# Attention outputs instead of softmax weights divided by the sums, with the reciprocals transposed on TensorE, in an encoder layer on one core

## The chip, the core and the metric

The kernel runs on one core of a Trainium2 chip. It has a matrix engine (TensorE, PE in the profile, with its weight loads as PEld), a vector engine (VectorE, DVE), a scalar engine (ScalarE, ACT), a general one (GpSimd, POOL), an engine that only issues transfers here (SyncE, SP), and 16 DMA engines. The metric is the device time of one execution, in microseconds (us).

## What is computed

One layer of an encoder in float32 for two requests, a prompt of 1024 tokens and a sample of 512, each of 1024 features, with tokens on a grid 64 columns wide (16 and 8 rows): normalization, attention of each query to a neighbourhood of up to 8 rows by 16 columns of keys, a residual, then normalization, a SwiGLU feed-forward of 2816 features, a residual and a last normalization. The attention has 16 heads of 64 features. Cut to what matters, per row of queries (rs is its first row of keys; kr and vr are 8 rows of keys and values in column bands of 32):

```python
s = einsum('bjqhd,bkjchd->bhjqkc', qr, kr) * scale
s = where(valid_j, s + bias, -inf)
p = softmax(s over all keys k, c)
return einsum('bhjqkc,bkjchd->bjqhd', p, vr)      # then o @ w_o
```

A softmax is exp(s - max) divided by its sum over the keys. That sum is one number for a query and a head, so the division can be made on the weights p, or later on the 64 outputs of that query and head.

## The kernel before

**Stages.** Until about 160 us tokens are normalized and transposed and the values V of all heads are projected, and stored in device memory. Then come the attention steps of the prompt (179 to about 520 us), those of the sample (to about 730 us) with the output projection between them, and then the feed-forward, which the change does not touch. Every float32 operand of a large product is split into a rounded part and a remainder (`split`, L138 on ACT and L139 on DVE; with a scale L141 and L142) and multiplied in three passes.

**A step.** A step is one pair of heads, one group of query rows and one of four blocks of 16 columns: 128 queries (8 rows by 16 columns) by 384 keys in the prompt, by 256 in the sample. The prompt has 8 pairs x 2 groups x 4 blocks = 64 steps, the sample 8 x 4 = 32. In a step

- `scores` multiplies queries by keys (pss, L394, 6 products on PE), adds the bias and finds the maximum (s and mx, L402, DVE, straight from PSUM), takes the exponential with its sum (s and sm, L405, ACT), inverts the sum (ri, L407, DVE) and multiplies the weights s by it, for head 0 on DVE (L409) and for head 1 on ACT (L411);
- `flip` transposes the weights on PE in blocks of 128x128 (ptt, L420, 3 per head in the prompt, 2 in the sample), copies the result rounded (pT, L423, ACT) and puts the remainder beside it (L424, DVE);
- `weighted` multiplies by V (po, L431): the outputs stand in PSUM with the features of a head on the partitions and the queries along the free axis, one bank per head and two steps beside each other;
- `collect`, every second step, adds the parts of po (tmp, L441 on ACT and L442 on DVE; oT, L444 on DVE) into oT, [128 features of two heads, 512 queries]; after the last block of a group a POOL transfer stores oT in device memory (o_d, L461).

**The order on the engines.** `step` (L476) writes the work of neighbouring steps interleaved: the scores of step t+1, the transposes of step t, then pieces of other products that keep PE busy, then the value products of step t. These pieces (`fillers`) are the q and k projections of the next pair (pg, L332, 12 products for a step), and in the sample also the output projection (pgo, L586). After each step `chores.do()` splits one piece that has been loaded (V of a row group: v from vr, four transfers at L378 on SP; weights of the next projection: whl from wr) and starts the next load; the buffers for these loads ("raw") are two, shared by both kinds, so a load starts only after the work on the one before. `fill_bias` keeps the bias tiles three ahead (bp, bs: transfers on SP, and for the prompt a memset on POOL, L204 and L208). The final order on each engine is set by the tile scheduler from this program and its estimates of durations; it, not only the text, moves rows when an instruction is added. PSUM has eight banks: two each for pss, ptt, po and pg.

## Time and profile before

| | |
|---|---|
| three timed runs | 1843.49, 1845.11, 1845.51 us (median 1845.11) |
| the profiled execution | 1845.18 us, span 1843.4 us |
| PE, PEld busy | 1754.1, 1522.5 us (95%, 83%) |
| DVE, ACT, POOL busy | 1192.9, 863.7, 448.4 us (65%, 47%, 24%) |
| mean DMA traffic | 151 GB/s |

Busy times are means over stages with different limits. In the views below L402 is line 402 of the kernel; "out<-in" are the program's names; a time "idle before" is how long the engine stood still before an instruction, and the name behind "<-" is what it waited for last. Windows give the busy time of each engine in a stretch of the span; the chain of waits follows the work that ended last back from instruction to releaser.

### The profile page before, as it was taken

The numbers are of one execution on the slowest core, as the hardware profiler recorded it, in microseconds if no ns is written. First come the engines' busy times: TensorE is split into PE (matmuls) and PEld (weight loads), VectorE is DVE, ScalarE is ACT, GpSimd is POOL, SyncE is SP. The second block draws the span as 40 slices with busy tenths as digits, with TensorE's granted clock in tenths as the row PEclk, the third lists the DMA queues.
The fourth block names the chain that finished last, engine by engine and source line by source line (L and its number), as shares of the span: only waits on it lengthen the run. The fifth ranks groups of instructions, "written<-read, shape, count | busy, mean of one in ns | idle before, by whom it ended". The sixth has DMA issues, their size and how long they took to land.

```text
span 1843.4 us, 25648 instructions
## 1 busy us (share of the span) xinstructions
PE 1754.1 (95%) x9178; PEld 1522.5 (83%) x9178; DVE 1192.9 (65%) x2191; ACT 863.7 (47%) x1706; POOL 448.4 (24%) x495
## 2 busy tenths in 40 slices
PE   8999999999999999979999999999999969999898
PEld 6877777777767777868999999899999958887676
DVE  4401877777896566768777777867777444545654
ACT  4411776766785554544443444444443333333322
POOL 1211000000130000112243342424243323526420
PEclk9999999999999999988999999999999979999999
DMA  7755334333464443676343434544333277635732
GB/s 245 221 183 160 111 105 113 108 101 103 126 208 146 133 149 100 221 247 185 108 121 118 133 110 151 164 129 125 108 120 107 68 272 245 225 130 191 232 129 100
DMA packets 222048, 278.80 MB, mean 151 GB/s; under 512 B 25600, under 2 KB 171776, under 8 KB 221920
## 3 DMA queue, kind: packets, MB, share of 16 engines
q1 hardware_dynamic: 201824, 210.69, 37.3%
q0 software_dynamic: 18368, 60.18, 9.5%
q10 hardware_dynamic: 1728, 6.29, 1.1%
q8 instruction: 72, 1.18, 0.3%
q14 instruction: 56, 0.46, 0.1%
HBM read 213.20 MB, written 76.43 MB: 157 GB/s over the span
## 4 chain that ended last, share of the span: by engine, by line
PE 68%; DVE 10%; DMA 9%; ACT 5%; issue 3%; SPq 2%; POOL 2%; DVEq 0%; ACTq 0%; POOLq 0%
PE pa L754 20%; PE pd L910 12%; PE pd L754 10%; PE pgv L278 7%; PE pg L332 6%; PE pb L754 5%; DMA vr<-v_d 5%; PE pgo L586 3%; DMA dr<-ffn_w_down 2%; PE pss L394 2%; PE ptt L420 2%; DVE pT L424 2%; SPq L378 2%; PE po L431 2%; ACT s L405 1%
## 5 line engine op out<-in xcount | busy, mean ns | idle before, releaser
L910 PE MATMUL pd<-wd,go 128*128 128x512 f32 x1386 | 323.0, 395 | 30.5 <-ACT go L138 20.4
L910 PEld LDWEIGHTS pd<-wd,go 128*128 128x128 f32 x1386 | 263.0, 191 | 90.4 <-ACT go L138 21.6
L754 PE MATMUL pa<-h,ws 128*128 128x384 f32 x1056 | 201.8, 339 | 2.9 <-ACT c L777 2.1
L754 PE MATMUL pa<-h,wa 128*128 128x384 f32 x1056 | 195.1, 338 | 7.0 <-ACT wa L138 4.5
L754 PE MATMUL pd<-h,ws 128*128 128x384 f32 x1056 | 198.3, 335 | 1.2 <-ACT h L138 0.6
L332 PE MATMUL pg<-hTp,whl 128*128 128x512 f32 x768 | 193.7, 399 | 0.0
L754 PEld LDWEIGHTS pa<-h,wa 128*128 128x128 f32 x1056 | 185.8, 190 | 8.9 <-ACT wa L138 5.2
L139 DVE TENSOR_TENSOR ws<-wt,ws 128x1024 fp32r<-128x1024 f32 x88 | 108.6, 1235 | 127.1 <-ACT ws L138 126.7
L754 PEld LDWEIGHTS pa<-h,ws 128*128 128x128 f32 x1056 | 185.1, 189 | 6.7 <-ACT c L777 4.3
L754 PEld LDWEIGHTS pd<-h,ws 128*128 128x128 f32 x1056 | 184.5, 188 | 1.8 <-ACT h L138 1.0
L332 PEld LDWEIGHTS pg<-hTp,whl 128*128 128x128 f32 x768 | 139.9, 188 | 27.5 <-issue 0.4
L805 POOL DMA_DIRECT2D gop_d<-c x66 | 50.5, 765 | 387.4 <-DVE c L796 380.3
L405 ACT ACTIVATE s<-s,mx 128x384 f32<-128x384 f32 (+1 forms) x192 | 110.7, 580 | 67.3 <-DVE mx L402 67.1
L586 PE MATMUL pgo<-wo,oh 128*128 128x512 f32 x576 | 139.3, 392 | 0.2 <-DVE oh L139 0.2
L139 DVE TENSOR_TENSOR wa<-wr,wa 128x512 fp32r<-128x512 f32 x132 | 117.8, 897 | 18.4 <-ACT wa L138 17.8
L138 ACT CAST ws<-wt 128x1024 fp32r<-128x1024 f32 x88 | 92.6, 1053 | 68.6 <-PE pd L754 65.4
L586 PEld LDWEIGHTS pgo<-wo,oh 128*128 128x128 f32 x576 | 105.6, 188 | 20.7 <-DVE oh L139 0.6
L138 ACT CAST go<-gr 128x1408 fp32r<-128x1408 f32 x42 | 57.7, 1374 | 131.2 <-PE pd L910 114.0
L138 ACT CAST wa<-wr 128x512 fp32r<-128x512 f32 x132 | 81.4, 621 | 62.8 <-PE pb L754 40.0
L754 PE MATMUL pb<-h,wa 128*128 128x384 f32 x528 | 102.0, 340 | 3.4 <-DVE c L774 3.4
L332 PE MATMUL pg<-hTs,whl 128*128 128x512 f32 x384 | 102.6, 404 | 0.8 <-DVE q L343 0.8
L424 DVE TENSOR_TENSOR pT<-ptt,pT 128x384 fp32r<-128x384 f32 (+1 forms) x192 | 90.0, 507 | 17.3 <-ACT pT L423 16.5
(138 smaller groups left out, 2859.6 us busy)
## 6 DMA issues: line engine op xcount, KB each, us to landing
gr<-gop_d SPq DMA_DIRECT2D x42, 704.0 KB
dr<-ffn_w_down SPq DMA_DIRECT2D x99, 256.0 KB
wr<-ffn_w_gate SPq DMA_DIRECT2D x44, 512.0 KB
wr<-ffn_w_up SPq DMA_DIRECT2D x44, 512.0 KB
wr<-na_w_qkv SPq DMA_DIRECT2D x38, 512.0 KB
gop_d<-gs POOLq DMA_DIRECT2D x88, 192.0 KB, 4.4
gop_d<-c POOLq DMA_DIRECT2D x66, 192.0 KB, 2.8
vr<-v_d SPq DMA_DIRECT2D x192, 64.0 KB
```

What stands on the lines that cost most here:

```text
L138: nc.scalar.copy(hi, raw)
L139: nc.vector.tensor_tensor(lo, raw, f32(hi), ALU.subtract)
L278: nc.tensor.matmul(pg, hh[a][:, k, c:c + P], wv[k // 2][b][:, k % 2], start=(k == 0 and i == 0), stop=(k == KB - 1 and i == 2))
L332: nc.tensor.matmul(pg, w[:, a, k, :], h[b][:, k, c:c + 512], start=(k == 0 and i == 0), stop=(k == KB - 1 and i == 2))
L378: nc.sync.dma_start(out=raw[:, j * P:(j + 1) * P], in_=src[:, BS[j]:BS[j] + 32, :])
L394: nc.tensor.matmul(pt[:, :n], q[h * HD:(h + 1) * HD, a, j].rearrange("p r i -> p (r i)"), kv[:, krow:krow + nrow, BS[j]:BS[j] + 32], start ...
L405: nc.scalar.activation(s[:, :n], s[:, :n], AF.Exp, bias=mx, scale=-1.0, accum_out=sm)
L424: nc.vector.tensor_tensor(pT[:, :n, 1], pv, f32(pT[:, :n, 0]), ALU.subtract)
L586: nc.tensor.matmul(pg, ohs[k // 4][:, a, k % 4], wo[:, b, k, n * 512:(n + 1) * 512], start=(k == 0 and i == 0), stop=(k == KB - 1 and i == 2))
L754: nc.tensor.matmul(bank[:, :HT], a(y, k), b[:, z, k], start=start and k == 0 and i == 0, stop=k == KB // 2 - 1 and i == 2, skip_group_chec ...
L805: nc.gpsimd.dma_start(out=gop_d[i, 3 * c:3 * c + 3, :, p].rearrange("j q t -> q j t"), in_=a.rearrange("q (j t) -> q j t", j=3))
L910: nc.tensor.matmul(pd, go[:, y, i], wds[i][:, z], start=(i == 0 and m == 0), stop=(i == NP - 1 and m == 2))
```

## The change

The weights s are no longer multiplied by the reciprocal. The sums of both heads go into the two columns of one tile sm; one reciprocal on DVE reads them 64 times each and writes ri, [128 queries, 2 x 64]. `flip` transposes ri after the transposes of head 1, into the free last quarter of the same PSUM bank: column by column it becomes [2 x 64 features, 128 queries], with the reciprocal of head 0 on partitions 0 to 63 and of head 1 on 64 to 127, which is the layout of oT. ACT copies it to rt, behind the cast of pT of head 1. Behind each `collect` POOL multiplies the two column blocks of oT that have just been written by their rt. Per step go two reciprocals of 128x1, one DVE and one ACT multiplication of the weights; come one reciprocal of 128x128, one transpose, one copy and (two every second step) one POOL multiplication of 128x128. The tile tmp serves both heads now and has one buffer in place of two; ri has one buffer, rt three. Lines of the changed kernel that differ: scores L403, exponential L405, reciprocal L408, transposes L418 and L420, the copy L427, value products L433, collect L443 to L446.

```diff
@@ -396,33 +396,35 @@
                                      start=(i == 0), stop=(i == 2))
             yield
             out = []
+            sm = stat.tile([P, 2], F32, tag="sm", name="sm")
             for h, pt in enumerate(pss):
                 s = ap.tile([P, 384], F32, tag="s", name="s", bufs=4)
                 mx = stat.tile([P, 1], F32, tag="mx", name="mx")
                 nc.vector.tensor_tensor_reduce(s[:, :n], pt[:, :n], bias(h), -1.0, 3.0e38,
                                                ALU.add, ALU.min, accum_out=mx)
-                sm = stat.tile([P, 1], F32, tag="sm", name="sm")
-                nc.scalar.activation(s[:, :n], s[:, :n], AF.Exp, bias=mx, scale=-1.0, accum_out=sm)
-                ri = stat.tile([P, 1], F32, tag="ri", name="ri")
-                nc.vector.reciprocal(ri, sm)
-                if h == 0:
-                    nc.vector.tensor_scalar(s[:, :n], s[:, :n], ri, None, ALU.mult)
-                else:
-                    nc.scalar.mul(s[:, :n], s[:, :n], ri)
+                nc.scalar.activation(s[:, :n], s[:, :n], AF.Exp, bias=mx, scale=-1.0, accum_out=sm[:, h:h + 1])
                 out.append(s)
-            yield out
-
-        def flip(ss, n):
+            ri = ap.tile([P, P], F32, tag="ri", name="ri", bufs=1)
+            nc.vector.reciprocal(ri.rearrange("p (h d) -> p h d", h=2),
+                                 sm.rearrange("p (h o) -> p h o", o=1).to_broadcast([P, 2, HD]))
+            yield out, ri
+
+        def flip(ss, n, ri, rt):
+
             out = []
-            for s in ss:
+            for h, s in enumerate(ss):
                 pt = psum("T", "ptt")
                 for c in range(n):
                     nc.tensor.transpose(pt[:, c * P:(c + 1) * P], s[:, c * P:(c + 1) * P], ident)
+                if h:
+                    nc.tensor.transpose(pt[:, 3 * P:], ri, ident)
                 pT = ap.tile([P, 3, 2, P], F32R, tag="pT", name="pT", bufs=3)
                 pv = pt[:, :n * P].rearrange("p (c q) -> p c q", q=P)
                 nc.scalar.copy(pT[:, :n, 0], pv)
                 nc.vector.tensor_tensor(pT[:, :n, 1], pv, f32(pT[:, :n, 0]), ALU.subtract)
                 out.append(pT)
+                if h:
+                    nc.scalar.copy(rt, pt[:, 3 * P:])
             return out
 
         def weighted(pT, vs, j, n, pos, g):
@@ -433,10 +435,10 @@
                                      start=(c == 0), stop=(c == n - 1))
 
         def collect(pos, dst):
+            tmp = ap.tile([P, 2, P], F32, tag="tmp", name="tmp", bufs=1)
             for h in range(2):
                 m, o = (0, HD) if h == 0 else (HD, 0)
                 pv = pos[h].rearrange("p (g z q) -> p g z q", g=2, z=2)
-                tmp = ap.tile([P, 2, P], F32, tag="tmp", name="tmp")
                 t = tmp[m:m + HD]
                 nc.scalar.copy(t, pv[o:o + HD, :, 0])
                 nc.vector.tensor_tensor(t, t, pv[m:m + HD, :, 0], ALU.add)
@@ -452,12 +454,15 @@
                 pos = []
                 for u in range(2):
                     j = jj * 2 + u
+                    last_rt = rt if u else None
+                    rt = ap.tile([P, P], F32, tag="rt", name="rt", bufs=3)
                     if j != 2:
                         b = next_bias()
                     yield dict(
                         s=lambda b=b, j=j: scores(q, k, 4 * (g == 1), 4 * n, j, lambda h: b[:, h, :n * P]),
-                        n=n, pos=pos, g=u, j=j, v=v,
+                        n=n, pos=pos, g=u, j=j, v=v, rt=rt,
                         dst=(lambda h, jj=jj: ov[h * HD:(h + 1) * HD, jj * 2:jj * 2 + 2]) if u else None,
+                        all=[(ov[:, j - 1], last_rt), (ov[:, j], rt)] if u else None,
                         done=(lambda: nc.gpsimd.dma_start(out=o_d[hp, :, g * 512:(g + 1) * 512], in_=oT))
                         if j == 3 else None)
                     fill_bias()
@@ -479,8 +484,8 @@
                 next(sc)
             pT = None
             if prev:
-                p, pss = prev.pop()
-                pT = flip(pss, p["n"])
+                p, (pss, ri) = prev.pop()
+                pT = flip(pss, p["n"], ri, p["rt"])
             ss = next(sc) if sc else None
             run(fillers, n)
             if pT:
@@ -489,6 +494,8 @@
                 weighted(pT, [x() for x in p["v"]], p["j"], p["n"], p["pos"], p["g"])
                 if p["dst"]:
                     collect(p["pos"], p["dst"])
+                    for a, r in p["all"]:
+                        nc.gpsimd.tensor_tensor(a, a, r.rearrange("p (r i) -> p r i", i=16), ALU.mult)
                 if p["done"]:
                     p["done"]()
             if st:
```

The following rows list the instructions of an engine in program order, by line, operation and tile; "x2" is a run of alike rows. First PE in an ordinary head pair of the prompt, from the value products of one step to the first products behind the transposes of the next, before

```order
L431 MATMUL po<-pT,v 128x256 x6
L394 MATMUL pss<-kp,q 128x384 x6
L420 MATMUL ptt<-ident,s 128x128 x3
L332 MATMUL pg<-hTp_102,whl 128x512
L420 MATMUL ptt<-ident,s 128x128 x3
L332 MATMUL pg<-hTp_103,whl 128x512
```

and with the change:

```order
L433 MATMUL po<-pT,v 128x256 x6
L394 MATMUL pss<-kp,q 128x384 x6
L418 MATMUL ptt<-ident,s 128x128 x6
L420 MATMUL ptt<-ident,ri 128x128
L332 MATMUL pg<-hTp_102,whl 128x512
L332 MATMUL pg<-hTp_103,whl 128x512
L332 MATMUL pg<-hTp_102,whl 128x512 x2
```

The transposes of the weights have become one run, the transpose of ri stands at its end, and the q/k projections (pg) stand behind it.

Second, ACT in the sample, over two steps in which q is rounded and weights of a projection (whl) are split, before

```order
L411 ACTIVATE s<-s,ri 128x256
L138 CAST v<-vr 128x4x2x64
L441 COPY tmp<-po 64x256 x2
L423 CAST pT<-ptt 128x2x128 x2
L405 ACTIVATE s,sm<-s,mx 128x256 x2
L411 ACTIVATE s<-s,ri 128x256
L342 CAST q<-pg 128x512
L141 ACTIVATE whl<-wr 128x1024
L423 CAST pT<-ptt 128x2x128 x2
```

and with the change:

```order
L427 COPY rt<-ptt 128x128
L138 CAST v<-vr 128x4x2x64
L443 COPY tmp<-po 64x256 x2
L423 CAST pT<-ptt 128x2x128
L405 ACTIVATE s,sm<-s,mx 128x256
L423 CAST pT<-ptt 128x2x128
L405 ACTIVATE s,sm<-s,mx 128x256
L427 COPY rt<-ptt 128x128
L342 CAST q<-pg 128x512
L141 ACTIVATE whl<-wr 128x1024
L423 CAST pT<-ptt 128x2x128
```

The multiplication L411 between the exponentials and the cast of q is gone, the copy to rt stands in its place, and the casts of pT and the exponentials alternate.

Third, DVE in the sample, around the remainder of whl (L139, 128x1024) that follows that of ks, before

```order
L424 TENSOR_TENSOR pT<-ptt,pT 128x2x128
L402 ISA s,mx<-pss,bs 128x256
L402 ISA mx 128x1
L424 TENSOR_TENSOR pT<-ptt,pT 128x2x128
L407 RECIPROCAL ri<-sm 128x1
L139 TENSOR_TENSOR v<-vr,v 128x4x128
L409 TENSOR_SCALAR s<-s,ri 128x256
L407 RECIPROCAL ri<-sm 128x1
L350 TENSOR_TENSOR ks<-pg,ks 128x512
L139 TENSOR_TENSOR whl<-wr,whl 128x1024
L424 TENSOR_TENSOR pT<-ptt,pT 128x2x128 x2
```

and with the change:

```order
L424 TENSOR_TENSOR pT<-ptt,pT 128x2x128 x2
L403 ISA s,mx<-pss,bs 128x256
L403 ISA mx 128x1
L403 ISA s,mx<-pss,bs 128x256
L403 ISA mx 128x1
L350 TENSOR_TENSOR ks<-pg,ks 128x512
L139 TENSOR_TENSOR v<-vr,v 128x4x128
L139 TENSOR_TENSOR whl<-wr,whl 128x1024
L408 RECIPROCAL ri<-sm 128x128
L424 TENSOR_TENSOR pT<-ptt,pT 128x2x128
```

The two reciprocals of 128x1 and the multiplication L409 before whl are gone; the reciprocal of 128x128 stands behind whl, before the subtractions of the next step's pT.

## The prediction

> **What bounds the kernel now.** I read the windows of the attention stages first, then the waits of the weight loads (PEld) that open a transpose or a value product, then the chain of waits in one head pair of the prompt and in the sample loop. The rest of the program (norm and V projection before 179 us, feed-forward after 735 us) keeps its instructions and is left out of the sum. The rows of the windows give the stretch, its length, and the busy time of PE, PEld, DVE, ACT and POOL, then the granted clock, the DMA share and GB/s.
>
> ```profile
> 179.00:520.00 341.00, 327.07 (x1868) 254.18 (x1866) 271.55 (x776) 243.62 (x589) 27.92 (x61) 1.00 0.39 113
> 520.00:735.00 215.00, 205.68 (x1097) 159.55 (x1095) 145.68 (x427) 124.75 (x323) 26.91 (x26) 1.00 0.46 141
> 485.00:530.00 45.00, 43.36 (x240) 31.59 (x237) 41.64 (x118) 39.59 (x94) 16.42 (x11) 1.00 0.49 154
> 266.00:309.00 43.00, 41.60 (x240) 32.61 (x238) 34.12 (x98) 30.08 (x74) 3.09 (x8) 1.00 0.37 107
> ```
>
> PE is busy for 96% of the prompt steps (first row, 64 steps) and of the sample steps (second row, 32 steps). It idles 341.00 - 327.07 = 13.9 us and 215.00 - 205.68 = 9.3 us: 23.2 us is all that any relief of DVE and ACT can win there. In an ordinary head pair (fourth row, 43 us) DVE has 8.9 us free; around the change from prompt to sample (third row) DVE is busy 41.64 of 45 us and has hardly any.
>
> Who PE waits for stands in the idle lists of the transposes (L420) and of the value products (L431); the numbers are us and times.
>
> ```profile
> L420 PEld LDWEIGHTS ptt<-ident,s x512: 137/140/143, 184.2 to 730.6; 128*128 128x128 f32 x171
> ...
>   ACT s L411: 14.5, 40
> ...
>   DVE ri L407: 5.5, 17
> ```
>
> ```profile
> L431 PEld LDWEIGHTS po<-pT,v x512: 186/188/192, 187.5 to 733.8; 128*128 128x128 f32 x171
> ...
>   DVE pT L424: 27.5, 35
> ```
>
> So two kinds of waits exist: for the softmax weights (the reciprocal and the multiplication by it, which the change removes from that path) and for the transposed weights pT (which the change touches only through DVE's and ACT's load). The chain of waits shows both in one head pair:
>
> ```profile
> 230.27 4.55 DMA vr<-v_d
> ...
> 234.92 0.62 ACT v L138
> ...
> 235.95 0.57 DVE pT L424
> ...
> 236.56 1.09 PE po L431 x6
> ...
> 244.39 0.53 ACT s L411
> ...
> 244.96 0.55 PE ptt L420 x3
> ```
>
> The first wait belongs to the loading of V (the cast of v stands ahead of that of pT on ACT); the second is the ACT multiplication that goes.
>
> **What it removes.** The durations below are smallest, median and largest ns.
>
> ```profile
> L407 DVE RECIPROCAL ri<-sm x192: 132/157/166, 183.1 to 729.2; 128x1 f32<-128x1 f32 x192
> ```
>
> ```profile
> L409 DVE TENSOR_SCALAR s<-s,ri x96: 341/416/2691, 183.3 to 728.9; 128x384 f32<-128x384 f32 x64, 128x256 f32<-128x256 f32 x32
> ```
>
> ```profile
> L411 ACT ACTIVATE s<-s,ri x96: 494/615/632, 184.5 to 729.3; 128x384 f32<-128x384 f32 x64, 128x256 f32<-128x256 f32 x32
> ```
>
> A step loses two reciprocals and one multiplication on DVE, 2 x 0.157 + 0.416 = 0.73 us, and 0.615 us on ACT.
>
> **What it adds on PE.** One transpose more per step. A run of six stands in the timeline of the weight loads, with two starts of neighbouring steps:
>
> ```profile
> 293.03 0.64 PEld L420 LDWEIGHTS ptt<-ident,s 128*128 128x128 f32 x6 [0.26 <-issue]
> 293.64 2.61 PEld L332 LDWEIGHTS pg<-hTp,whl 128*128 128x128 f32 x12
> ...
> 297.31 0.47 PEld L394 LDWEIGHTS pss<-kp,q 64*128 64x128 f32 x6
> ...
> 302.33 0.47 PEld L394 LDWEIGHTS pss<-kp,q 64*128 64x128 f32 x6
> ```
>
> Six transposes take 0.61 to 0.64 us, 0.105 each. An unstalled prompt step is 302.33 - 297.31 = 5.02 us of back-to-back work, so the transpose is paid in full: 96 x 0.105 = **10.1 us**, 6.7 in the prompt and 3.4 in the sample. Only idle that goes can pay it back.
>
> **What it adds on DVE.** One reciprocal of 128x128 per step, a form the trace does not hold. Its lower bound is a reciprocal that streams like other work. For that the two forms of the score reduction and a one-element operation of another kind:
>
> ```profile
> L402 DVE CUSTOM_DVE_ANT_0 s<-pss,bp x128: 535/548/559, 181.8 to 518.5; 128x384 f32<-128x384 f32 x128
> ...
> L402 DVE CUSTOM_DVE_ANT_0 s<-pss,bs x64: 403/419/427, 521.6 to 727.0; 128x256 f32<-128x256 f32 x64
> ```
>
> ```profile
> L117 DVE TENSOR_SCALAR me<-ms x24: 144/152/155, 6.3 to 833.1; 128x1 f32<-128x1 f32 x24
> ```
>
> The slope is (548 - 419) / 128 = 1.01 ns an element, so 0.157 + 127 x 0.00101 = 0.29 us at least. But one element of reciprocal takes 5 ns (medians) to 11 ns (largest) more than one element of the other operation. If that excess comes with every element, it is 0.29 + 127 x 0.005 = 0.92 to 0.29 + 127 x 0.011 = 1.69 us. A fixed excess of an instruction would look the same in these rows, so both ends stay open; I take 1.2 us, nearer to the medians' end, because an excess of a few ns on a single element looks like the work on that element. Then a step's DVE work changes by -0.73 + 1.2 = **+0.47 us**; at the lower bound by -0.44.
>
> The Trainium skill bears on this choice: "VectorE: DVE Perf Modes", section "First, the fixed hardware budget", says that the reciprocal is an iterative divide with a repeat count of 8. Eight cycles for each of 128 elements at that page's 0.96 GHz are an estimated 1.07 us and a fixed part, which would give the slow sum below; by the streaming slope the fast rival's sum holds. No row here shows a reciprocal of more than one element.
>
> **What it adds on ACT and POOL.** The casts of L423 and the multiplications on POOL are the nearest rows:
>
> ```profile
> L423 ACT CAST pT<-ptt x192: 348/475/488, 185.0 to 731.3; 128x384 fp32r<-128x384 f32 x128, 128x256 fp32r<-128x256 f32 x64
> ```
>
> ```profile
> L800 POOL TENSOR_TENSOR gs<-c 128x384 f32<-128x384 f32 x22 | 24.0, 1089 | 34.4 <-DVE c L796 34.4
> ```
>
> The copy of 128x128 by that slope is 0.475 - 2 x 0.127 = 0.22 us, so ACT gains 0.39 us a step. It waits for the subtraction of head 1 (same bank), and the next exponential is queued behind it; ACT has 43.00 - 30.08 = 12.9 us free in the fourth window, so I cost that wait at nothing, and at the copy's 0.22 us a step if the cover is gone. A multiplication on POOL is at most a third of 1.089, 0.36 us, and a little fixed time: 0.4 us, 96 times, on an engine busy for 3 of 43 us. Behind it on POOL stand the bias memsets, the stores of the attention outputs and, in the sample, the stores of x1; all have over 1 us to spare, so that is nothing.
>
> **The sum, stage by stage (reciprocal at 1.2 us).** PE +10.1. Ordinary prompt head pairs: the waits for weights end sooner, because transposes no longer wait for 0.157 + 0.615 after the last exponential but the seventh transpose for 1.2 us, and six transposes (0.63 us) run in that time: 1.2 - 0.63 - 0.77 = -0.2 us, about once per head pair, -2 over the stage. Against that, 8 x 0.47 = 3.8 us more DVE work per head pair, most of it in the 8.9 us free; what falls ahead of a wait for pT shows. I take 0.4 us per head pair, less than one reciprocal's excess, 7 x 0.4 = +2.8; its ends are 0 and one excess at each of the two kinds of waits, 7 x 0.94 = 6.6. The full stretch, 485 to 530 us: 9 steps x 0.47 = 4.2 us on 41.64; kept at its present 92.5% busy it lasts 45.9 / 0.925 = 49.6, +4.6, of which 0.9 is the transposes already counted and some is free again in what follows: +3. The sample loop:
>
> ```profile
> 595.27 4.37 DMA vr<-v_d
> ...
> 604.16 0.08 DVE ri L407
> ...
> 604.27 0.35 DVE s L409
> ...
> 604.62 0.08 DVE ri L407
> ...
> 604.73 0.51 ACT s L411
> 605.24 0.48 ACT q L342
> 605.71 0.97 ACT whl L141
> 606.71 1.24 DVE whl L142
> ...
> 609.67 4.39 DMA vr<-v_d
> ...
> 639.69 4.75 DMA vr<-v_d
> ```
>
> From one load of V to the next is (639.69 - 595.27) / 3 = 14.8 us for two steps, set by this loop (buffer of the load, V, outputs, scores, weights of the next pair, buffer), not by PE, which idles 9.3 / (215 / 14.8) = 0.64 us in it. The change takes 0.08 + 0.35 + 0.08 + 0.51 = 1.02 us out of the loop and adds a copy of 0.22 on ACT and a reciprocal of 1.2 on DVE (it stands behind whl in the rows shown of the order, but then ahead of the next pT and outputs, so I charge it once per loop), about even: the loop stays near 14.8, and its 3.4 us of transposes go into idle time, -3.4. In all 10.1 - 2 + 2.8 + 3 - 3.4 = **+10.5 us**. The profiled execution took 1845.18 us (median of the runs 1845.11), so 1855.7, say **1856**.
>
> **Rivals.**
>
> *A: the reciprocal streams (0.29 us).* Then everything moves the change's way: DVE falls by 0.44 us a step, waits for weights go, and the sample loop loses 1.02 - 0.29 - 0.22 = 0.5 us, down to about 14.4, PE's own 14.2 + 0.2. Of 13.9 us of idle in the prompt about 6 stay by my estimate (the wait at 236.56 us for the loading of V, once per head pair), so 8 go; of 9.3 in the sample 6 go: 10.1 - 14 = -4, 1841, and down to 1836 if the waits for V shorten too. It decides where the reciprocal costs under 0.73 us, what it replaces. For it: a single element is no proof of a rate. Against: those 5 to 11 ns. It forecasts faster, just outside 0.2% (3.7 us, about what a measurement of this kernel can tell from no change).
>
> *B: all is hidden.* The slow reciprocal falls into DVE's free time, and the removed multiplications take the idle that the transposes fill: 10.1 against 2 + 3.4 and another 4 from the waits for pT: 1846. For it: 23 us of idle; against: the full stretch, where DVE has none free.
>
> *C: POOL holds DVE.* While POOL ran a 128x1024 subtraction, DVE's operations between SBUF tiles took far longer:
>
> ```profile
> 519.93 1.22 DVE L142 SCALAR_TENSOR_TENSOR whl<-wr,whl 128x1024 fp32r<-128x1024 f32 x1
> ...
> 522.27 2.21 DVE L139 TENSOR_TENSOR whl<-wr,whl 128x1024 fp32r<-128x1024 f32 x1
> ```
>
> and the 2691 ns of L409 fall there too. The multiplications put 96 x 0.4 = 38 us on POOL inside the loops; if a third of that is added to DVE ahead of a wait, and half of that shows, 6 us more: 1862, to 1868 with the reciprocal at 1.69. Against it: right behind the outputs DVE mostly works from PSUM.
>
> **How the numbers follow.** The forecast (1849 to 1860) has 0.51, A 0.24, B 0.14, C 0.11. Most of A and a little of B lie under 1841.4, so faster is 0.24; B's middle and A's upper end make same 0.17; the forecast and C make slower 0.59. The range leaves out the far end of A and the top of C: 1837 to 1866. The forecast's own range is 1849 to 1860.
>
> **What would show it.** The row of the reciprocal: over 0.9 us, or 0.29 (then A). The window of the prompt should hold 6.7 us more PE time, and PEld rows of seven transposes of 0.73 us. The waits of transposes for ACT's multiplication should be gone, with waits for the reciprocal in their place; DVE busy in the stretch at 485 us should be over 45 us. I am wrong if the two stages together get shorter, or if the loads of V in the sample come closer than 14.6 us.

## The result, and the profile after

The changed kernel takes 1862.01 us (median of four runs, 1861.73 to 1864.51), the kernel before 1845.16: the ratio is 1.0096, with a 95% interval of 1.0079 to 1.0114, so about 17 us slower. The profiled execution took 1861.73 us, its span is 1859.9.

The time is followed along PE, by the first and last start (the two numbers behind the durations) of four groups of products: the V projection (pgv), the q/k projections that run beside the attention (pg), the value products (po) and the feed-forward (pa, pd); hTp are the tokens of the prompt, hTs those of the sample. First the kernel before, the operations of a source line with smallest, median and largest ns:

```profile
L278 PE MATMUL pgv<-wv,hTp x384: 388/393/795, 9.9 to 134.6; 128*128 128x512 f32 x192
L278 PE MATMUL pgv<-wv,hTs x192: 390/393/477, 64.7 to 157.0; 128*128 128x512 f32 x192
...
L332 PE MATMUL pg<-hTp,whl x768: 387/390/498, 157.2 to 482.4; 128*128 128x512 f32 x192
L332 PE MATMUL pg<-hTs,whl x384: 387/393/507, 485.4 to 709.2; 128*128 128x512 f32 x192
...
L431 PE MATMUL po<-pT,v x512: 274/283/388, 187.7 to 733.9; 128*128 128x256 f32 x171
...
L754 PE MATMUL pa<-h,wa x1056: 334/334/689, 810.1 to 1481.3; 128*128 128x384 f32 x176
...
L910 PE MATMUL pd<-wd,go x1386: 387/389/796, 1498.7 to 1834.7; 128*128 128x512 f32 x198
```

The same of the changed kernel:

```profile
L278 PE MATMUL pgv<-wv,hTp x384: 387/389/797, 9.5 to 132.3; 128*128 128x512 f32 x192
L278 PE MATMUL pgv<-wv,hTs x192: 390/393/475, 63.6 to 154.6; 128*128 128x512 f32 x192
...
L332 PE MATMUL pg<-hTp,whl x768: 387/393/505, 154.8 to 484.0; 128*128 128x512 f32 x192
L332 PE MATMUL pg<-hTs,whl x384: 387/393/507, 486.9 to 715.0; 128*128 128x512 f32 x192
...
L433 PE MATMUL po<-pT,v x512: 274/282/389, 186.0 to 740.7; 128*128 128x256 f32 x171
...
L761 PE MATMUL pa<-h,wa x1056: 333/337/689, 816.3 to 1492.6; 128*128 128x384 f32 x176
...
L917 PE MATMUL pd<-wd,go x1386: 387/393/795, 1509.4 to 1851.7; 128*128 128x512 f32 x198
```

| | before | changed | difference |
|---|---|---|---|
| start to first pgv | 9.9 | 9.5 | -0.4 |
| V projection (first pgv to first pg) | 147.3 | 145.3 | -2.0 |
| attention (first pg to last po) | 576.7 | 585.9 | +9.2 |
| rest of the span (feed-forward) | 1109.5 | 1119.2 | +9.7 |
| span | 1843.4 | 1859.9 | +16.5 |

The attention gets 9.2 us longer; the prediction said 10.5. But the feed-forward, in which not one instruction was changed, gets 9.7 us longer, and the V projection ahead of everything 2.0 us shorter. The medians already show it: a product of pa ends 337 ns after its start in place of 334, one of pd (L910, now L917) 393 in place of 389, one of pgv over hTp 389 in place of 393. The q/k projection of the prompt goes from 390 to 393; the products over hTs stay at 393.

In the attention itself, first the new instructions:

```profile
L408 DVE RECIPROCAL ri<-sm x96: 939/953/955, 181.9 to 735.2; 128x128 f32<-128x128 f32 x96
```

```profile
L498 POOL TENSOR_TENSOR oT<-oT,rt x96: 444/463/1436, 194.7 to 743.5; 128x128 f32<-128x128 f32 x96
```

```profile
L427 ACT COPY rt<-ptt x96: 243/266/270, 186.2 to 739.3; 128x128 f32<-128x128 f32 x96
...
  DVE pT L424: 31.1, 53
  POOL oT L498: 12.2, 7
```

The reciprocal takes 0.953 us, six times that of one element. The multiplication on POOL takes 0.46, the copy on ACT 0.27, and ACT stands 31.1 us before it, waiting for DVE's subtraction, and another 12.2 us in seven waits for the multiplication on POOL. A step without stalls, in the timeline of the weight loads, with the seventh transpose behind the six:

```profile
297.23 0.47 PEld L394 LDWEIGHTS pss<-kp,q 64*128 64x128 f32 x6
297.96 0.64 PEld L418 LDWEIGHTS ptt<-ident,s 128*128 128x128 f32 x6 [0.26 <-issue]
298.57 0.14 PEld L420 LDWEIGHTS ptt<-ident,ri 128*128 128x128 f32 x1
298.68 2.62 PEld L332 LDWEIGHTS pg<-hTp,whl 128*128 128x128 f32 x12
301.34 0.90 PEld L433 LDWEIGHTS po<-pT,v 128*128 128x128 f32 x6
302.38 0.47 PEld L394 LDWEIGHTS pss<-kp,q 64*128 64x128 f32 x6
```

It lasts 302.38 - 297.23 = 5.15 us; before it was 5.02. What the weight loads wait for over the attention, as us, times and longest, in the kernel before (178 to 735 us):

```profile
PEld po L431 <- DVE pT L424: 17.6, 21, 1.8
PEld ptt L420 <- issue: 17.2, 57, 1.3
PEld ptt L420 <- ACT s L411: 11.7, 32, 0.9
...
PEld ptt L420 <- PE pss L394: 7.9, 16, 0.7
```

and in the changed one (178 to 742 us):

```profile
PEld po L433 <- DVE pT L424: 22.5, 41, 2.3
...
PEld ptt L418 <- issue: 10.5, 43, 0.3
PEld ptt L420 <- DVE ri L408: 7.7, 20, 0.5
PEld ptt L418 <- ACT s L405: 4.6, 17, 0.4
```

The wait for ACT's multiplication (11.7 us) has gone, as it should; in its place stand shorter waits for the exponential and for the new reciprocal (12.3 together), and the value products wait for pT twice as often. But the other waits of the transposes have shrunk as well: "issue" from 17.2 to 10.5, and the 7.9 for the scores are gone. With the waits of PE itself, all waits in front of transposes come to 46.7 us before (L420) and 26.9 with the change (L418 and L420). PE as a whole idles less over the steps, 548.00 - 524.75 = 23.2 us before,

```profile
179.00:727.00 548.00, 524.75 (x2922) 407.11 (x2920) 412.36 (x1186) 364.32 (x899) 54.29 (x86) 1.00 0.42 125
```

and 554.00 - 540.30 = 13.7 us with the change:

```profile
179.00:733.00 554.00, 540.30 (x3006) 419.09 (x3004) 437.47 (x994) 338.75 (x896) 99.60 (x178) 1.00 0.41 124
```

Short waits need not show as idle time of PE: in the profile a transpose lasts 273 ns, while back to back they start 0.11 us apart. So we also count in another way: each product gets the time from the start of the product before it to its own start, its wait included. Summed over the attention (first pg to last po, us):

| | before | changed | difference | e1, a run below |
|---|---|---|---|---|
| transposes (512; 608) | 98.0 | 96.7 | -1.3 | 96.7 |
| value products | 89.2 | 94.3 | +5.1 | 93.5 |
| scores | 72.5 | 75.2 | +2.7 | 75.5 |
| q/k projection, prompt | 167.6 | 173.0 | +5.4 | 170.9 |
| q/k projection, sample | 84.3 | 82.0 | -2.3 | 82.1 |
| output projection | 65.0 | 64.7 | -0.3 | 64.7 |

The 96 transposes more cost nothing in this count, because the transposes wait less; the attention gets longer behind them, at the value products, the scores and the projections. These are single executions: in e12 below, which does the same as the kernel before, the first row is 95.7 and the second 90.8.

### The profile page after: what moved, and what is told of

The parts are those of the page before. It is cut to its first block, busy times and chain, and to the rows that moved or that the text cites. A ratio compares the mean times of both kernels' runs of the same rounds, so it can differ in the third digit from the quotient of the medians.

```text
span 1859.9 us, 26013 instructions
## 1 busy us (share of the span) xinstructions
PE 1784.4 (96%) x9274; PEld 1546.3 (83%) x9274; DVE 1220.0 (66%) x1999; ACT 839.7 (45%) x1706; POOL 496.9 (27%) x591
## 4 chain that ended last, share of the span: by engine, by line
PE 60%; DMA 9%; DVE 8%; ACT 3%; issue 3%; SPq 1%; POOL 1%; DVEq 0%; ACTq 0%; POOLq 0%
PE pa L761 19%; PE pd L917 13%; PE pd L761 9%; PE pgo L593 5%; PE pb L761 5%; DMA vr<-v_d 4%; PE pg L332 4%; PE pss L394 1%; DVE pT L424 1%; DMA dr<-ffn_w_down 1%; PE ptt L418 1%; PE po L433 1%; SPq L378 1%; DVE s L403 1%; ACT s L405 1%
## 5 line engine op out<-in xcount | busy, mean ns | idle before, releaser
L917 PE MATMUL pd<-wd,go 128*128 128x512 f32 x1386 | 331.2, 401 | 28.0 <-ACT go L138 19.1
L917 PEld LDWEIGHTS pd<-wd,go 128*128 128x128 f32 x1386 | 264.8, 192 | 94.2 <-ACT go L138 19.9
L139 DVE TENSOR_TENSOR ws<-wt,ws 128x1024 fp32r<-128x1024 f32 x88 | 109.3, 1244 | 131.0 <-ACT ws L138 129.6
L139 DVE TENSOR_TENSOR wa<-wr,wa 128x512 fp32r<-128x512 f32 x132 | 117.8, 897 | 19.5 <-ACT wa L138 18.9
L405 ACT ACTIVATE s<-s,mx 128x384 f32<-128x384 f32 (+1 forms) x192 | 111.2, 580 | 22.5 <-DVE mx L403 21.2
L424 DVE TENSOR_TENSOR pT<-ptt,pT 128x384 fp32r<-128x384 f32 (+1 forms) x192 | 93.9, 508 | 33.9 <-ACT pT L423 32.7
L498 POOL TENSOR_TENSOR oT<-oT,rt 128x128 f32<-128x128 f32 x96 | 47.7, 518 | 235.7 <-DVE oT L446 147.1
L408 DVE RECIPROCAL ri<-sm 128x128 f32<-128x128 f32 x96 | 91.2, 950 | 25.8 <-ACT s L405 24.4
```

The source lines that it names most:

```text
L139: nc.vector.tensor_tensor(lo, raw, f32(hi), ALU.subtract)
L405: nc.scalar.activation(s[:, :n], s[:, :n], AF.Exp, bias=mx, scale=-1.0, accum_out=sm[:, h:h + 1])
L408: nc.vector.reciprocal(ri.rearrange("p (h d) -> p h d", h=2), sm.rearrange("p (h o) -> p h o", o=1).to_broadcast([P, 2, HD]))
L424: nc.vector.tensor_tensor(pT[:, :n, 1], pv, f32(pT[:, :n, 0]), ALU.subtract)
L498: nc.gpsimd.tensor_tensor(a, a, r.rearrange("p (r i) -> p r i", i=16), ALU.mult)
L917: nc.tensor.matmul(pd, go[:, y, i], wds[i][:, z], start=(i == 0 and m == 0), stop=(i == NP - 1 and m == 2))
```

## The experiments

Two questions were open. What made unchanged products slower: PLACEMENT (the addresses of their operands) or PHASE (the stream of instructions, or the moment at which a stage starts)? And what made the attention longer: the RECIPROCAL on DVE, the ACT QUEUE behind the copy to rt, or the transposes alone? For the first, the built programs tell where each buffer lies. The small pool `stat` had four slots of 32 bytes for ri before and has none for it now; all pools opened after it on that side lie 128 bytes lower. Buffers on the other side (hTp, ws, wa, wd, wo) did not move. Addresses modulo 256 bytes, moving operand / stationary operand:

| product | before | changed | PE's pace before, changed |
|---|---|---|---|
| V projection of the prompt, wv / hTp | 0 / 128 | 128 / 128 | slower, faster |
| V projection of the sample, wv / hTs | 0 / 128 | 128 / 0 | slower, slower |
| q/k projection of the prompt, hTp / whl | 128 / 128 | 128 / 0 | faster, slower |
| q/k projection of the sample, hTs / whl | 128 / 128 | 0 / 0 | the same |
| up, h / ws and wa | 128 / 128 | 0 / 128 | faster, slower |
| down, wd / go | 128 / 128 | 128 / 0 | faster, slower |

Ratios below are to the kernel before on the same chip, whose single times spread over some 6 to 13 us there; a difference of 2 to 3 us between two experiments is within their intervals. One execution of the kernel before, of 7924.5 us, is left out. The runs that only move buffers (e1 beside the changed kernel; e2, e5, e11 and e12 beside the kernel before) have the same instructions in the same order on every engine, so in them addresses are all that differs. In e3, e4 and e6 to e10 the tile scheduler also put other rows elsewhere: in e3, for one, 354 of the 3148 products of the attention stand in another place than in e1. What these gain or lose belongs to the edit together with that order.

**e1: the changed kernel at the old addresses.**

```diff
-        ident = cpool.tile([P, P + 24], F32, name="ident")[:, :P]
+        ident = cpool.tile([P, P + 56], F32, name="ident")[:, :P]
```

> The changed kernel with 128 bytes of padding behind the identity tile, which puts the buffers of V projection and feed-forward back to the SBUF addresses of the kernel before (the change had moved them down by 128 bytes, because a tile of four 32-byte slots went); the instructions are the same. Theory PLACEMENT (PE's pace in unchanged products depends on where their operands lie): the feed-forward loses the 10 us that it gained and the V projection gives back its 2.4, 1862 - 10.3 + 2.4 = 1854. Rival PHASE (PE's pace is set by the instruction stream or by the moment at which a stage starts): 1862, as the changed kernel.

Measured: 1855.24 us beside 1843.41, ratio 1.0062 (1.0041 to 1.0084), against 1.0096 without the padding. In the profile the V projection takes 147.6 us again, the rest 1109.7 again (before: 147.3 and 1109.5), the attention 583.4. The intervals of e1 and of the changed kernel (1.0079 to 1.0114) just overlap, so the stages and the counts below decide, and e2. PLACEMENT holds. How PE's pace looks in windows: number of up products (first row, 950 to 1050 us) and of down products (1530 to 1590 us) started in a stretch in which PE never stops, at a granted clock of 1.00; columns are PE, PEld, clock, DMA share, GB/s. The kernel before:

```profile
950.00:1050.00 100.00, 100.00 (x576) 99.39 (x576) 1.00 0.41 125
```

```profile
1530.00:1590.00 60.00, 60.00 (x266) 49.67 (x266) 1.00 0.73 257
```

The changed kernel:

```profile
950.00:1050.00 100.00, 100.00 (x570) 99.97 (x569) 1.00 0.35 110
```

```profile
1530.00:1590.00 60.00, 60.00 (x260) 48.65 (x259) 1.00 0.72 250
```

e1, with the same instructions as the changed kernel:

```profile
950.00:1050.00 100.00, 100.00 (x577) 99.55 (x576) 1.00 0.36 113
```

```profile
1530.00:1590.00 60.00, 60.00 (x266) 49.73 (x265) 1.00 0.74 252
```

PE is busy for 100% in all six, so no wait shows; only the count tells: 576 products of 384 columns in 100 us against 570 (174 and 175 ns each), 266 of 512 columns in 60 us against 260 (226 and 231 ns).

**e2: the kernel before, moved by 128 bytes.** The same edit as e1, in the kernel before.

> The kernel before, with nothing but the same 128 bytes of padding, so its buffers move by 128 bytes the other way. PLACEMENT: if the place counts by multiples of 256 bytes, the feed-forward gets slower by 10 us and the V projection faster by 2.4, 1845.2 + 8 = 1853; if the place counts in another way, some other time clear of 1845. PHASE: 1845, no change.

Measured: 1854.1 us beside 1843.41, ratio 1.0056 (1.0036 to 1.0075). Of the kernel before, without any change in what it does, a gap of 128 bytes makes a kernel that is 10 us slower. Its windows:

```profile
950.00:1050.00 100.00, 100.00 (x570) 99.99 (x569) 1.00 0.38 126
```

```profile
1530.00:1590.00 60.00, 60.00 (x260) 48.65 (x259) 1.00 0.72 251
```

The counts are those of the changed kernel, 570 and 260. With the instructions and their order unchanged, PHASE has fallen. The attention takes 577.0 us in this profile (576.7 before): there the slower q/k projection costs nothing that shows.

**e3: the reciprocal made small.** On e1:

```diff
+            rs2 = ap.tile([P, 2], F32, tag="rs2", name="rs2", bufs=2)
+            nc.vector.reciprocal(rs2, sm)
             ri = ap.tile([P, P], F32, tag="ri", name="ri", bufs=1)
-            nc.vector.reciprocal(ri.rearrange("p (h d) -> p h d", h=2),
-                                 sm.rearrange("p (h o) -> p h o", o=1).to_broadcast([P, 2, HD]))
+            nc.vector.tensor_copy(ri.rearrange("p (h d) -> p h d", h=2),
+                                  rs2.rearrange("p (h o) -> p h o", o=1).to_broadcast([P, 2, HD]))
```

> The padded changed kernel; DVE inverts the two sums of a query (128x2) and spreads the result by a copy to 128x128, in place of the reciprocal of 128x128. DVE work per step falls by 0.95 - 0.16 - 0.2 = 0.6 us. Theory RECIPROCAL (the 0.95 us on DVE make the attention stages longer): the attention loses 4 to 8 of its 9 us, 1846 to 1850. Rival ACT QUEUE (the copy to rt waits for DVE's subtraction and holds the exponentials behind it): within 2 us of the padded kernel, 1852 to 1854.

Measured: 1841.97 us beside 1843.41, ratio 0.9994 (0.9979 to 1.0010): 13 us less than e1 (6 to 19 by the ends of the intervals), more than expected. By the profiles the attention is 9.5 us shorter than in e1 (573.9), and the rest, where nothing differs, 5.3 us (1104.4), the lowest of all runs. The two instructions that replace the 0.953 us:

```profile
L408 DVE RECIPROCAL rs<-sm x96: 148/166/168, 183.4 to 725.2; 128x2 f32<-128x2 f32 x96
```

```profile
L410 DVE COPY ri<-rs x96: 210/227/4333, 183.6 to 725.4; 128x128 f32<-128x128 f32 x96
```

DVE does 0.953 - 0.166 - 0.227 = 0.56 us less per step, 54 us over 96 steps, and the kernel is 13 us shorter: about a quarter of DVE's time shows. The value products wait less for pT: 23.2 us in 43 waits of PE and PEld, where e1 has 30.7 in 56. ACT QUEUE falls as the main cause, since ACT stands before the copy to rt as long as it did:

```profile
L429 ACT COPY rt<-ptt x96: 243/266/278, 187.5 to 729.4; 128x128 f32<-128x128 f32 x96
...
  DVE pT L426: 33.9, 52
```

RECIPROCAL holds in its direction; how much of the 13 us is the reciprocal and how much the order of the rows moved with it, no run separates. One of the copies took 4.33 us; at that place POOL subtracted two tiles of 128x1024, in the timelines of DVE and POOL:

```profile
525.28 4.33 DVE L410 COPY ri<-rs 128x128 f32<-128x128 f32 x1
```

```profile
524.83 4.69 POOL L524 TENSOR_TENSOR wo<-or,wo 128x1024 fp32r<-128x1024 f32 x2
```

**e4: the copy to rt ahead of the subtraction.** On e1:

```diff
+                if h:
+                    nc.scalar.copy(rt, pt[:, 3 * P:])
                 nc.vector.tensor_tensor(pT[:, :n, 1], pv, f32(pT[:, :n, 0]), ALU.subtract)
                 out.append(pT)
-                if h:
-                    nc.scalar.copy(rt, pt[:, 3 * P:])
```

> The padded changed kernel; the copy to rt stands ahead of DVE's subtraction of head 1, so ACT does not wait for DVE there (DVE waits for 0.27 us of ACT instead). ACT QUEUE: the 31 us that ACT stood before that copy go, and the attention gets 3 to 5 us shorter, 1849 to 1851. RECIPROCAL: within 1.5 us of the padded kernel, 1853 to 1855.

Measured: 1852.63 us beside 1843.41, ratio 1.0045 (1.0028 to 1.0062), 2.6 us below e1 with intervals that overlap by about half of their width or more, and between the two ranges. In its profile the attention is not shorter than in e1 (586.0 us). The edit exchanges one wait for another: ACT no longer waits there, but DVE's subtraction waits for the copy, longer than the 0.27 us of one copy:

```profile
L425 ACT COPY rt<-ptt x96: 263/273/287, 186.1 to 740.7; 128x128 f32<-128x128 f32 x96
...
  DVE pT L426: 16.5, 25
```

So what ACT's 31.1 us before that copy are worth, this test cannot say; it shows only that this order wins at most a few us.

**e5: only the V projection moved, in the kernel before.**

```diff
-            fill = vp.tile([P, 480], F32, tag="fill", name="fill", bufs=1)
+            fill = vp.tile([P, 512], F32, tag="fill", name="fill", bufs=1)[:, :480]
```

> The kernel before with one unused gap of 128 bytes ahead of the weights of the V projection alone, so that these weights (wv) and the tokens (hTp) lie at the same address modulo 256 bytes; no other buffer moves. Theory PLACEMENT, made sharper by the first runs (a product runs at PE's clean pace when its two operands have the same address modulo 256 bytes, and 1.4 to 2.7% slower when they lie 128 bytes apart): the V projection falls from 233 to 229 ns or less per product, 2.3 us shorter, 1841 where the kernel before takes 1843.4. Rival: no change (what it gains, a later load takes back): within 1 us.

Measured: 1840.71 us beside 1844.22, ratio 0.9985 (0.9975 to 0.9995). As expected. V products over hTs, which the change had left slow, are fast here too, 389 ns in the median in place of 393:

```profile
L278 PE MATMUL pgv<-wv,hTs x192: 387/389/476, 64.1 to 154.4; 128*128 128x512 f32 x192
```

V products started from 40 to 140 us in the kernel before:

```profile
40.00:140.00 100.00, 95.50 (x403) 74.81 (x402) 1.00 0.64 195
```

and in e5:

```profile
40.00:140.00 100.00, 95.40 (x411) 76.22 (x411) 1.00 0.62 195
```

**e6: the small reciprocal, spread by ACT.** The changed kernel with rs2 as a tile of `stat` (its four slots bring the old addresses back), and

```diff
+            nc.vector.reciprocal(rs2, sm)
-            nc.vector.reciprocal(ri.rearrange("p (h d) -> p h d", h=2),
-                                 sm.rearrange("p (h o) -> p h o", o=1).to_broadcast([P, 2, HD]))
+            nc.scalar.copy(ri.rearrange("p (h d) -> p h d", h=2),
+                           rs2.rearrange("p (h o) -> p h o", o=1).to_broadcast([P, 2, HD]))
```

> The changed kernel at the old addresses, sums inverted as 128x2 on DVE (0.166 us), spread to 128x128 by a copy on ACT instead of DVE. DVE does 0.57 us less per step than in the kernel before. RECIPROCAL: as good as the copy on DVE or 1 to 3 us better, 1839 to 1842, since DVE's copy was once held for 4.3 us while POOL worked. ACT QUEUE: 0.27 us more on ACT per step in front of waiting casts, 3 or more us slower, 1845 and above.

Measured: 1835.73 us beside 1844.22, ratio 0.9959 (0.9944 to 0.9973), faster than the kernel before by 8 us and better than expected. In an ordinary head pair, the window of 266 to 309 us (columns as in the prediction), e1 shows

```profile
266.00:309.00 43.00, 41.48 (x238) 32.55 (x237) 34.79 (x80) 26.68 (x73) 6.92 (x16) 1.00 0.35 101
```

and e6

```profile
266.00:309.00 43.00, 42.97 (x262) 34.92 (x260) 32.09 (x85) 31.23 (x87) 6.54 (x16) 1.00 0.38 110
```

PE starts 262 products in place of 238 in the same time and has no idle left; DVE is busy 2.7 us less, ACT 4.6 us more. One window of one execution says less than the whole stage: e9 below, with the same instructions in the attention, starts 252 there. The attention takes 567.0 us in the profile, 573.6 in e9 (e1: 583.4). ACT could carry the spread: ACT QUEUE falls for it.

**e7: no division at all.** On e1, without reciprocal, its transpose, copy and multiplications.

> The changed kernel at the old addresses without any division: no reciprocal, no transpose of it, no copy, no multiplication, so the attention outputs are not normalized. It shows what the removed instructions are worth alone. Theory RELIEF (the waits of PE for weights and for pT go with them; 23.2 us of idle is the limit): 12 to 18 us shorter than the kernel before, 1825 to 1831. Rival V LOADS (most of the idle belongs to the loads of V): 4 to 8 us shorter, 1835 to 1839.

Measured: 1829.24 us beside 1844.22, ratio 0.9931 (0.9913 to 0.9949), 15 us less by the medians, 13 by the ratio. RELIEF holds: the attention takes 560.2 us in the profile where the kernel before takes 576.7, and PE's idle time over the steps falls from 23.0 to 10.5 us.

**e8: no division, one more transpose.** On e7:

```diff
+                if h:
+                    nc.tensor.transpose(pt[:, 3 * P:], s[:, :P], ident)
```

> The same without any division, but with one more transpose per step on PE (of a block of the weights, its result unused), 96 in all. Theory PE BOUND: 0.125 us a step (the unstalled step of the changed kernel took 5.14 where it took 5.02), 10 to 12 us more than without. Rival IDLE TAKES IT: 2 to 6 us more than without.

Measured: 1837.38 us beside 1844.22, ratio 0.9964 (0.9954 to 0.9975). The transposes cost 8.1 us by the medians and 6 by the ratios, between what the two theories said. Neither is shown: 96 x 0.13 = 12.5 us of transposes cost less than their own time by these medians, but the ends of the two intervals allow anything from 1 to 11 us, and the order of the rows differs too.

**e9 and e10: e6 with the placement of e5, and that with the copy of e4.**

> The version of e6 (sums inverted as 128x2, spread on ACT, old addresses) with the placement of e5 for the V projection. If the two are independent: 1835.7 - 3.5 = 1832, 12 us less than the kernel before. Rival (one takes what the other gave): 1835 to 1837.

> e9 with the copy to rt ahead of DVE's subtraction of head 1. ACT QUEUE, in its weak form (ACT carries the spread now, so its wait for DVE counts): 2 to 4 us less than e9. RECIPROCAL: that wait costs nothing once DVE is relieved, within 1.5 us of e9.

Measured, beside 1844.49: e9 1835.51 us, ratio 0.9952 (0.9939 to 0.9966), e10 1835.25, ratio 0.9951 (0.9936 to 0.9966). The V projection of e9 did get shorter (144.6 us in its profile, 147.1 in e6), but the sum of 1832 did not come; the time is the rival's (1835 to 1837): the attention of that execution took 573.6 us where that of e6 took 567.0, at the same instructions. Whether the later stages wait for loads that the earlier start does not move, or whether this is the scatter of single executions, stays open. e10 is no better than e9: once DVE is relieved, the order of copy and subtraction is worth nothing that these runs can tell.

**e11 and e12: the kernel before, moved by 64 and by 256 bytes** (P + 40 and P + 88 in place of P + 24 in the edit of e1).

> The kernel before with its buffers moved by 64 bytes, so that the operands of the feed-forward lie 64 bytes apart modulo 256 and those of the V projection 64 in place of 128. PLACEMENT as a matter of a 128-byte half (64 apart is as bad as 128, or as good as 0): a feed-forward pace of 176.1 or of 173.7 ns a product and nothing between. If it goes by distance: about 175 ns, 1848 to 1850.

> The kernel before with its buffers moved by 256 bytes. PLACEMENT modulo 256 bytes: no change, 1844, 173.7 ns a product in the feed-forward. Rival (any move of those buffers against the unmoved ones costs, the period is longer): 1850 or more.

Measured, beside 1844.49: e12 1844.39 us, ratio 0.9998 (0.9987 to 1.0009), no change: the place counts modulo 256 bytes. e11 1854.38, ratio 1.0060 (1.0046 to 1.0074), but not as either expectation had it:

```profile
950.00:1050.00 100.00, 100.00 (x577) 99.38 (x576) 1.00 0.40 126
```

```profile
1530.00:1590.00 60.00, 60.00 (x258) 48.34 (x258) 1.00 0.74 255
```

With operands 64 bytes apart the up products of 384 columns keep the clean pace (577) and the down products of 512 columns run slower than at 128 bytes (258). So there is no simple rule by distance; that equal places are clean is all that these runs show. One other reading fits V projection and feed-forward as well: that an operand at 0 modulo 256 is slow by itself. The q/k projection of the sample speaks against it. Its operands go from 128 / 128 to 0 / 0 with the change and keep their pace (medians of 393 ns in both, in the lists of the result), while the same products in the prompt, at 128 / 0, get slower.

## Why the prediction was right or wrong

**The direction and the costs of single instructions: right.** The unstalled step was forecast to grow by 0.105 us and grew by 0.13. The reciprocal was put between 0.92 and 1.69 us by the excess on a single element, with 1.2 taken; it measured 0.953, at the end that the medians gave. The slope from 1 to 128 elements is (953 - 157) / 127 = 6.3 ns an element, close to the 6 ns that a streamed element and the excess of 5 ns make together: the guess that the excess comes with every element was borne out. The Trainium skill's "VectorE: DVE Perf Modes", section "First, the fixed hardware budget", puts the reciprocal down to an iterative divide with a repeat count of 8. Eight cycles at that page's 0.96 GHz would be 8.3 ns, and the measured 6.3 ns is an estimated six; so the runs agree that the cost grows with every element, but not on eight cycles. A step's DVE work grew by 0.953 - 0.73 = 0.22 us in place of the forecast 0.47.

**The sum for the attention: near, and in part by luck.** The forecast of 10.5 us was 10.1 for the transposes less 2 for the waits for weights, 5.8 for waits behind DVE (2.8 and 3), and 3.4 back in the sample. The changed kernel's attention is 9.2 us longer; at the old addresses (e1) it is 583.4 - 576.7 = 6.7 us longer in one profile, and by e1's ratio the whole kernel is 11.4 us slower (7.6 to 15.5), so 10.5 cannot be told from what came. But the terms are others. The relief was mis-sized: the prediction's own lists have 14.5 + 5.5 = 20.0 us of waits of the transposes for ACT's multiplication and for the reciprocal, and it counted a gain of 2; the waits in front of transposes fell by 19.8 us (46.7 to 26.9), and with them the transposes paid for themselves (98.0 us before, 96.7 after). What came behind them was mis-sized the other way: value products, scores and the q/k projection of the prompt took 13.2 us more, of which about 2 belong to the addresses (173.0 against 170.9 us in e1), where the prediction had 5.8. The two errors largely offset each other.

The full stretch at 485 us, which was to have DVE at its limit, shows it at 37.51 of 45 us and not 92.5% busy:

```profile
485.00:530.00 45.00, 43.96 (x241) 33.05 (x241) 37.51 (x84) 32.62 (x81) 12.61 (x16) 1.00 0.46 141
```

The step of the prediction that kept DVE "at its present 92.5% busy" failed, and the claim that DVE would be busy for over 45 us of that stretch with it. The waits point to another way in which the slow reciprocal costs time: it stands ahead of the subtractions that the value products wait for (22.5 us on pT in place of 17.6, in 41 waits in place of 21), and e3, where it is gone, has fewer of these waits. That is argued from the waits; the order of the rows, which e3 changes too, is the rival left.

One sign that the prediction gave for being wrong did come: loads of V in the sample closer than 14.6 us. In the middle of the sample they start at 603.26, 616.40, 629.74 and 644.25 us, 13.7 us apart. The sample's steps still did not get shorter (218.0 us from their first scores to the last value product, 215.8 before, 216.0 in e1), so this distance was no good measure of the stage.

**"The rest of the program keeps its instructions and is left out of the sum": the step that failed.** The instructions were the same, but a pool that lost a tile moved the buffers behind it by 128 bytes. That is 9.7 us in the feed-forward and -2.0 in the V projection, 7.7 of the 16.5 us, and more than the 6 us by which the time lies above the forecast of 1856. e1 takes it away, e2 makes it without the change. The measured time lies outside the forecast's own range (1849 to 1860) and inside the wide one (1837 to 1866), which had been drawn for other reasons.

**Rival A** was wrong for this kernel, since the reciprocal does not stream, but right on what would decide: its point of 0.73 us on DVE. With 0.166 us on DVE and the spread on ACT (e6) the change is faster than before, at a ratio of 0.9959 (0.9944 to 0.9973), 8 us; A gave 4 to 9. **Rival B** (all is hidden, 1846) is out: e1 alone is above it. **Rival C**, that POOL holds DVE by the new multiplications, has little weight, though its 1862 is the number that came: e6 keeps all 96 of them, at about 0.46 us, and gains. What POOL did hold in the changed kernel is ACT, 12.2 us before the copy to rt; with the same multiplications it is 0.9 us in e6, and what it cost is not known. That POOL can hold DVE is real (a copy of 0.227 us took 4.33), but by the large subtractions that were there before.

**The wait at the copy, costed at nothing:** ACT does stand there for 31.1 us. In e3 it stands there for 33.9 and the kernel is 13 us shorter, so this wait is not what made the attention longer; whether it costs a few us stays open.

**What the change consists of, then:** without the division the kernel is 13 to 15 us shorter (e7), the transposes take 6 to 8 back (e8), copy, spread and POOL multiplication almost nothing beyond (e6), and the reciprocal of 128x128 another 13 (e3) to 19 (e6, with the spread on ACT), all at the old addresses. Each of these is a difference of two runs whose rows stand in different order, and good to a few us only.

## What to carry to other kernels

Dividing the outputs in place of the weights takes work off the path, but ask in which shape the reciprocal is made: here, inverting two numbers and spreading them by a copy took 0.39 us on DVE, and inverting the spread 128 took 0.95. Before a sum is made of what a change adds, add up all waits in front of the instructions whose inputs it brings forward. When a tile is added or dropped in a pool that opens early, compare the addresses of all later buffers: a stage that was not touched can change its pace. If a busy engine is 100% busy before and after, count its instructions in a window; that shows a pace that no wait explains.

## What the runs showed of the hardware

- PE's pace in products of the same shape, clock and neighbours depends on the addresses of its two operands modulo 256 bytes: equal places ran at 174 ns (384 columns) and 226 (512), 128 bytes apart at 175 and 231 (1.0% to 2.3% of a stage that is all PE). 256 bytes of shift made no difference; at 64 bytes apart 384 columns ran at 173 and 512 at 233. What makes it so is not shown.
- A reciprocal on DVE costs 6.3 ns an element beyond its fixed part (157, 166 and 953 ns for 1, 2 and 128 elements), where a copy of 128 elements takes 227 ns in all.
- A copy on DVE between SBUF tiles stood for 4.33 us while POOL worked on SBUF, and the same copy on ACT never took more than 0.32. The Trainium skill's "SBUF — State Buffer", section "Who interferes with whom", says that DVE and GpSimd share a pair of ports under an exclusive lock; the trace agrees, in that the copy ended 0.1 us after the second of POOL's two subtractions (525.28 + 4.33 and 524.83 + 4.69 us).
